# Two-layer hybrid encoder on one core: a weight sum, memory's operand and a low part drawn later, and one head's scaling on another engine

## The chip, the core and the metric

The kernel runs on one core of a Trainium2 chip. Its engines work side by side, each with its own queue in program order: TensorE (PE: matmuls and transposes; PEld is its weight load), VectorE (DVE), ScalarE (ACT), GpSimd (POOL) and SyncE (SP, which here only issues transfers). An instruction starts when everything ahead of it in its queue has been started and what it reads and writes is free. The metric is the device time of one execution in microseconds (us); lower is better.

## What is computed

The input is x, 512 tokens by 1024, and 256 memory tokens by 1024. There are two layers, all in 32-bit floats. Layer 0 attends in dilated windows (24 heads of 128 in three groups of eight), layer 1 with grouped queries (8 query heads on 2 key heads, rotated along two axes). Both also attend to memory with 4 heads. One projection of the normalised x feeds heads, memory queries and a SiLU gate; the gated heads go through an output projection and are added to x.

```
for i in range(DEPTH):
    h = rmsnorm(x, norm_g[i])
    mem_h = rmsnorm(mem, mem_norm_g[i])
    proj = jnp.einsum('bsd,de->bse', h, w_in)
...
    o_mem = memory_attention(q_mem, mem_h, w_mem_kv[i], mem_qn_g[i], mem_kn_g[i])
    y = jnp.concatenate([o_mix, o_mem], axis=-1) * jax.nn.silu(gate)
    x = x + jnp.einsum('bse,ed->bsd', y, w_out[i])
```

In layer 0 the three groups of a head are weighed against each other by a softmax over their log-sums: o = sum over g of w_g * o_g. The kernel keeps the scores of a head in two tiles `prob[o]` of 128 x 4 x 256: the first group (o = 0) and the two dilated ones side by side (o = 1).

## The kernel before

**Products in three passes.** A matmul of full 32-bit precision is made of three: each operand is split into a high part (rounded to the format fp32r) and a low part (what is left). `mm_early` and `mm_late` (L172, L173, L176) issue them: high by high, low by high, then high by low. For a weight, ScalarE draws the high part `wh` (L307, a cast of a 128x1024 piece) and VectorE the low part `wo` (L317, a subtraction). Activations are split the same way, by `split` (L160, L163) and by `put` (L567, L568).

**Seven products for eight.** Most projections (kinds W2, W1, W1b and their like) use a scheme of seven block products: the weights' quarters 21, 11, 12, 22 are combined into sums T1, T2, T3, T4. They are used in the order 21, 11, T1, T2, 22, T3, T4, each against one combination of activations (`PRODUCTS`: "12", "11", "S1", "S2", "S4", "S3", "22"). `s_chunk` runs them. Two accumulation banks take turns: the product with S2 is added to the bank of product 11, after `add` (L401) has read that bank, and the product with S4 to the bank of S1, after `keep` (L384) has.

**Weights.** The class `Weights` keeps the order of all this by hand. A step is one call of `advance`, made after each group of matmuls. In a step it draws low parts that are due (`lo`), issues at most one sum (`sum`), draws one or two high parts (`hi`), and issues loads (`dma`, on SP's queue, L258) as long as fewer pieces are live than `KEEP` says. T1 is summed on VectorE in layer 0 (L276) and by an adding transfer in layer 1 (L272); T2, T3 and T4 are adding transfers, issued by GpSimd (L281, L286, L291). T2 and T4 add one tile in on-chip memory to another (`wl<-wl`), T3 a piece of `wall`. A sum is issued no earlier than `LEAD` = 2 steps after the one that it needs; T4 needs T2 and the tile of quarter 21, whose low part must have been drawn one step before. A piece's tile is given back when its last user has been issued.

**Side work.** `Driver` runs everything else as generators, a piece of each per tick; a tick follows each step. `spawn(gen, n)` starts one n ticks later, and a `yield n` lets n ticks pass. `late` puts a piece at the end of the tick. The tiles of 128x1024 floats (tag m4: weights, activations, memory's tiles) share 23 places.

**Order around the change.** The list `PLAN` is worked through as `SEQ` orders it: memory's keys and values of layer 0 (8 steps), the plain values (14), memory's queries (7, chunk 3), the eight heads (14 each; head 0 is chunk 4), three gate chunks (7 each), the output projection (14, chunk 15, steps 162 to 175) with its last quarter (O1: 8 steps, 176 to 183), then layer 1: memory's keys and values (T2b: 8), memory's queries (W1bs: 7, chunk 20, steps 192 to 198), the rest (W1b, W2b, O1).

- Memory's queries (`ev_qm`): squares summed on ScalarE (L592), mse and rstd on GpSimd (L448, L449), the multiply on VectorE (L597), four transposes (L1073).
- `attn_a(h)` is the attention of head h of layer 0, spread over ticks. Its end: the factors `c`, `scale(1)`, two ticks later `scale(0)` and `turn(1)` (eight transposes, L1244), then `turn(0)`, `pv(1)` (L1265) and `pv(0)`. Head 7's end falls into the output projection, where VectorE also prepares the operands y (`prep_y`: L875, L890 to L905, casts L874).
- `mem_norm(1)`, spawned as the output projection begins, loads memory and its gains (L617, L634), four ticks later multiplies the first half (L495, two of them), one tick later the second half, and transposes and splits both (L501, L160, L163) in this and the next tick. Its result is read by the T2b steps.
- `rest_t` forms the activations S2, S4, S3, 22 of layer 1 (L571, L577; split by L567, L568) while the T2b and W1bs steps run.

Of the kernel before, what the change touches and what calls it, by code (L numbers as in the profile page):

```python
# [12 lines left out]
AF = mybir.ActivationFunctionType  # L13
ALU = mybir.AluOpType
# [7 lines left out]
TCKW = {}  # L22
NBIG, NM4, NS2, SCRATCH = 7, 23, 14, 2048
RING, LEAD = 4, 2
BULK, ACTIVE, SET_AT, WARM, MEM_B, PREP_Y, ACC_AT, PREP_B, HALF, SET_B = 2, 2, 15, 1, 12, 1, 4, 1, {"a": 3, "b": 3, "o": 0}, 9
MEM_STEP = 1, 1
MEM_D = 4
DIRECT, DIRECT_B = (7,), (6, 7)
# [8 lines left out]
PLAN = ["W2"] + ["T2"] * 2 + ["W1", "W2s"] + ["W2" if c.isdigit() else "W1" for c in A_ORDER[1:]] + ["W2"] + ["O1"] * 2 + ["T2b"] * 2 + ["W1bs"] + ["W1b"] * 6 + ["W2b"] + ["O1"] * 2  # L37

SEQ = [1, 2, 0] + list(range(3, len(PLAN)))
T1_DMA = 17  # L40
KEEP = {"T2": 8, "T2b": 6, "O1": 6, "W1": 9, "W2": 10, "W2s": 9, "W1bs": 9, "W1b": 7, "W2b": 9}

# [85 lines left out]
def trunk_kernel(ctx: ExitStack, tc: tile.TileContext, x, mem, wall, norm_g, mem_norm_g, gcol,  # L128
                 qn_a, kn_a, qn_b, kn_b, ident_d, mask_d, tab_a, tab_b, out):
    nc = tc.nc  # L130
    V, A, G, T = nc.vector, nc.scalar, nc.gpsimd, nc.tensor
# [11 lines left out]
    def m4(dt=F32, name="m4"):  # L143
        return pool.tile([128, 1024], dt, tag="m4", name=name, bufs=NM4)
# [43 lines left out]
    def pieces(kind):  # L188

        return 2 * GROUPS[kind][0] if kind in GROUPS else 4 if kind in ("W1", "W1b", "W1bs") else 8  # L190

    class Weights:
        def __init__(self):
            self.items, self.last, self.need, self.allocs, self.sums = [], [], [], [], []
            self.users = {}
            g = 0
            for c in SEQ:
                kind, d = PLAN[c], sum(pieces(k) for k in PLAN[:c])
                base = len(self.items)
                if kind in GROUPS:  # L200
                    units, nb = GROUPS[kind]
                    if kind == "O1":
                        n = PLAN[c - 1] == "O1"
                        for x in range(2):
                            self.items.append((c, "P", x))
                            self.last.append(g + 5)
                            self.allocs.append(((c, "P", x), d + x, kind))
                            self.users[c, "P", x] = 1
                        self.need += [base + 2] * 2 if not n else [base + 2] * 6
                        g += 2 if not n else 6  # L210
                        units = 0
                    for u in range(units):
                        for x in (2 * u, 2 * u + 1):
                            self.items.append((c, "P", x))
                            self.last.append(g + (u + 1) * nb - 1)
                            self.allocs.append(((c, "P", x), d, kind))
                            self.users[c, "P", x] = 1
                            d += 1
                        self.need += [base + 2 * u + 2] * nb
                    g += units * nb  # L220
                else:
                    n = 1 if kind in ("W1", "W1b", "W1bs") else 2
                    at = {k: d + i * n for i, k in enumerate(("21", "11", "12", "22"))}
                    self.allocs += [((c, k, x), at[q] + x, kind) for k, q in LOADS for x in range(n)]
                    for k in ORDER:
                        for x in range(n):
                            self.items.append((c, k, x))
                            self.last.append(g)
                            self.need.append(len(self.items))
                            if k[0] == "T":  # L230
                                self.sums.append(((c, k, x), at["11" if k == "T1" else "22"] + x))
                            if k != "T4":
                                self.users[c, k, x] = 1 if k in ("22", "T3") or k == "11" and c >= T1_DMA else 2
                            g += 1
            assert sum(pieces(k) for k in PLAN) == wall.shape[0]
            self.g = -1
            self.live = 0
            self.tile, self.load_at, self.at, self.lo_at = {}, {}, {}, {}
            self.n_hi = self.n_lo = self.taken = 0
            self.op, self.hi_at = [], []  # L240
# [22 lines left out]
        def sum(self, force=False, want=None):  # L263

            for n, (key, d) in enumerate(self.sums[:8]):
                if want and key != want:
                    continue
                c, k, x = key
                if k == "T1" and c >= T1_DMA:
                    if not self.ripe(self.load_at, key, force):  # L270
                        continue
                    G.dma_start(self.tile[key], wall[d], accum_op=ALU.add)  # L272
                elif k == "T1":
                    if not (self.ripe(self.load_at, key, force) and self.ripe(self.at, (c, "11", x), force)):
                        continue
                    V.tensor_tensor(self.tile[key], self.tile[key], self.tile[c, "11", x], ALU.add)  # L276
                    self.use((c, "11", x))
                elif k == "T2":
                    if not (self.ripe(self.load_at, key, force) and self.ripe(self.at, (c, "T1", x), force, 1 if c < T1_DMA else None)):
                        continue  # L280
                    G.dma_start(self.tile[key], self.tile[c, "T1", x], accum_op=ALU.add)  # L281
                    self.use((c, "T1", x))
                elif k == "T3":
                    if not self.ripe(self.load_at, key, force):
                        continue
                    G.dma_start(self.tile[key], wall[d], accum_op=ALU.add)  # L286
                else:
                    if not (self.ripe(self.lo_at, (c, "21", x), force, 1) and self.ripe(self.at, (c, "T2", x), force)):
                        continue
                    self.tile[key] = self.tile[c, "21", x]  # L290
                    G.dma_start(self.tile[key], self.tile[c, "T2", x], accum_op=ALU.add)  # L291
                    self.use((c, "T2", x))
                self.at[key] = self.g
                self.sums.pop(n)
                return True
            return False

        def hi(self, force=False):
            i = self.n_hi
            if i >= len(self.items) or not self.ripe(self.at, self.items[i], force, 1 if self.items[i][1] == "T1" and self.items[i][0] < T1_DMA else None):  # L300
                return False
# [31 lines left out]
        def advance(self):  # L333

            self.g += 1
            for _ in range(2):
                if self.n_lo < self.n_hi and self.hi_at[self.n_lo] < self.g:
                    self.lo()
            self.sum()
            if self.hi():  # L340
                self.hi()
            self.dma()
            if self.g + 1 < len(self.need):
                self.ready(self.need[self.g + 1])
# [787 lines left out]
    def attn_a(h, qk0, qs, ks, v12, n_done):  # L1132
# [3 lines left out]
        prob = [m4(name="p").rearrange("p (b k) -> p b k", b=4) for _ in range(2)]  # L1136
# [10 lines left out]
        for o in range(2):  # L1147
            new = []
            for b2 in range(2):
                sp = at("sa").rearrange("p (b k) -> p b k", b=2)  # L1150
                mine = []
                for i in range(2):
                    b = 2 * b2 + i
                    cs = slice(b * 128, (b + 1) * 128)
                    if o == 0:
                        lo, hi = max(0, 128 * b - 64), min(S, 128 * b + 192)
                        c0 = lo - (128 * b - 64)
                        c1 = c0 + hi - lo
                        T.matmul(sp[:, i, c0:c1], qk0[:, 0, cs], qk0[:, 1, lo:hi], start=True, stop=True, skip_group_check=True)  # L1159
                    else:  # L1160
                        c0, c1 = 0, 256
# [58 lines left out]
        V.reciprocal(rd, dn)  # L1220
        c = small.tile([128, 2, 4], F32, tag="c", name="c", bufs=2)
        V.tensor_tensor(c.rearrange("p o b -> p (o b)"), e[:, 0], rd, ALU.mult)
        yield 1

        pts = {}
# [2 lines left out]
        def scale(o):  # L1228
            for b in range(4):
                c0, c1 = (64 if o == 0 and b == 0 else 0), (192 if o == 0 and b == 3 else 256)  # L1230
                V.tensor_scalar(prob[o][:, b, c0:c1], prob[o][:, b, c0:c1], c[:, o, b:b + 1], 0.5, ALU.mult, ALU.mult)

        def turn(o):

# [24 lines left out]
        def pv(o):  # L1259
# [19 lines left out]
            drv.late(comb)  # L1279

        scale(1)
        yield Y[6]
        scale(0)
        turn(1)
        yield Y[7] + (h == 7)
# [10 lines left out]
    for c in A_ORDER:  # L1296
        if c.isdigit():
            drv.later(attn_a(int(c), *head_chunk(int(c))))
        else:
            if c == "b":  # L1300
                drv.spawn(prep_y(), PREP_Y)
            gate(H, *{"m": (8, 0), "a": (0, 1), "b": (4, 2)}[c])
# [334 lines left out]
```

## Time and profile before

| | us |
|---|---|
| median of 3 runs | 959.88 |
| lowest, highest | 959.16, 960.65 |
| profiled execution | 960.29 |
| span of its trace (first to last instruction) | 958.4 |

The granted TensorE clock was 1.000 over the whole span. The largest groups of the page are VectorE's low parts and ScalarE's high parts, then the matmuls:

```profile
L317 DVE TENSOR_TENSOR wo<-wl,wh 128x1024 fp32r<-128x1024 f32 x255 | 316.0, 1245 | 5.6 <-ACT wh L307 5.5
L307 ACT CAST wh<-wl 128x1024 fp32r<-128x1024 f32 x255 | 268.5, 1059 | 34.5 <-PE pj L173 16.9
L172 PE MATMUL pj<-wh,hS 128*128 128x512 f32 (+1 forms) x448 | 157.4, 365 | 1.6 <-ACT hS L567 1.6
```

How to read the rows. A group gives line, engine, operation, output<-inputs, shapes, count, then the busy time in us and the mean of one in ns, then the idle time of the engine just ahead of it and what ended most of that. A row of waits gives the waiting instruction, what released it, the total in us, how often, and the longest. A row of the timeline gives start and duration in us, then the instruction or a run of like ones (x3), and in brackets the idle time before it. Each duration overlaps the next one's start a little. A releaser is inferred from what ended last and can be another than the true one. An engine that waits costs nothing unless the one that sets the end waits for it.

### The profile page before, as it was taken

How to read it: one execution, taken by the hardware profiler on the slowest of the kernel's cores; microseconds unless marked ns; L12 is line 12 of the kernel's file. 1: busy time of each engine (PE TensorE's matmuls, PEld its weight loads, DVE VectorE, ACT ScalarE, POOL GpSimd, SP SyncE). 2: the span in 40 equal slices, each digit the busy share in tenths (PEclk: the TensorE clock that was granted, in tenths of full speed). 3: DMA queues.
4: the chain of work that ended last, by engine and by line, in shares of the span. 5: the costliest groups of instructions: out<-in, count | busy, mean ns of one | idle time of the engine just before them, and what ended most of it. 6: DMA issues, size and time to landing. Idle time of an engine off the chain costs nothing.

```text
span 958.4 us, 16597 instructions
## 1 busy us (share of the span) xinstructions
PE 944.6 (99%) x5682; PEld 831.9 (87%) x5682; DVE 791.7 (83%) x1415; ACT 678.0 (71%) x1693; POOL 332.7 (35%) x478
## 2 busy tenths in 40 slices
PE   8999999999999999999999999999999999999998
PEld 4879888888888888888889997878999999998886
DVE  4999586888888888979788999977988898769893
ACT  5875689686868686767775766537778876879770
POOL 1412423557454546463726111113232330011110
PEclk9999999999999999999999999999999999999999
DMA  9989946868787969696877989889885687787824
GB/s 354 320 193 344 304 111 173 291 133 258 152 260 156 262 154 264 154 259 138 234 185 185 268 204 308 280 250 328 230 189 117 190 237 173 210 207 187 248 54 127
DMA packets 87897, 208.23 MB, mean 217 GB/s; under 512 B 25219, under 2 KB 35203, under 8 KB 87813
## 3 DMA queue, kind: packets, MB, share of 16 engines
q1 hardware_dynamic: 68660, 144.18, 44.1%
q0 software_dynamic: 17856, 60.83, 34.2%
q10 hardware_dynamic: 1296, 2.16, 0.6%
q8 instruction: 45, 0.74, 0.3%
q14 instruction: 40, 0.32, 0.1%
HBM read 156.48 MB, written 11.86 MB: 176 GB/s over the span
## 4 chain that ended last, share of the span: by engine, by line
PE 90%; DVE 4%; DMA 3%; ACT 2%; issue 1%; POOL 0%; DVEq 0%; ACTq 0%; POOLq 0%
PE pj L173 24%; PE pj L172 23%; PE pj L176 23%; PE qT L604 2%; PE pt L1244 2%; PE sa L1163 1%; PE oo L1265 1%; PE sa L1159 1%; PE ptb L1467 1%; DMA og<-odb 1%; DVE wo L317 1%; PE xT L501 1%; PE ob L176 1%; PE row L625 1%; PE pmt L734 1%
## 5 line engine op out<-in xcount | busy, mean ns | idle before, releaser
L317 DVE TENSOR_TENSOR wo<-wl,wh 128x1024 fp32r<-128x1024 f32 x255 | 316.0, 1245 | 5.6 <-ACT wh L307 5.5
L307 ACT CAST wh<-wl 128x1024 fp32r<-128x1024 f32 x255 | 268.5, 1059 | 34.5 <-PE pj L173 16.9
L172 PE MATMUL pj<-wh,hS 128*128 128x512 f32 (+1 forms) x448 | 157.4, 365 | 1.6 <-ACT hS L567 1.6
L173 PE MATMUL pj<-wh,hS 128*128 128x512 f32 (+1 forms) x448 | 152.0, 353 | 0.0
L172 PE MATMUL pj<-wh,h 128*128 128x512 f32 (+1 forms) x336 | 117.9, 364 | 0.0
L173 PE MATMUL pj<-wh,h 128*128 128x512 f32 (+1 forms) x336 | 114.0, 353 | 0.0
L449 POOL TENSOR_TENSOR rstd<-mse,half 128x4 f32<-128x4 f32 (+2 forms) x96 | 100.5, 1046 | 8.0
L176 PE MATMUL pj<-wo,hS 128*128 128x512 f32 (+1 forms) x448 | 100.0, 352 | 0.2 <-DVE wo L317 0.2
L172 PEld LDWEIGHTS pj<-wh,hS 128*128 128x128 f32 x448 | 84.8, 189 | 12.1 <-ACT wh L307 1.8
L173 PEld LDWEIGHTS pj<-wh,hS 128*128 128x128 f32 x448 | 84.9, 190 | 10.2
L384 ACT COPY sn<-pj 128x512 f32<-128x512 f32 x132 | 73.2, 590 | 25.9 <-PE pj L176 23.7
L176 PEld LDWEIGHTS pj<-wo,hS 128*128 128x128 f32 x448 | 74.6, 189 | 12.4 <-DVE wo L317 0.6
L448 POOL TENSOR_SCALAR mse<-hss 128x4 f32<-128x4 f32 (+1 forms) x86 | 42.4, 493 | 123.0 <-ACT junk L592 118.6
L592 ACT ACTIVATE junk<-sn 128x128 f32<-128x128 f32 x264 | 79.1, 308 | 4.8 <-DVE sn L395 4.7
L1107 POOL TENSOR_TENSOR ta<-sn,tabs 128x128 f32<-128x128 f32 (+1 forms) x64 | 36.6, 579 | 119.5 <-DVE sn L597 92.4
L401 DVE TENSOR_TENSOR sn<-pj,sn 128x512 f32<-128x512 f32 x99 | 67.3, 683 | 9.2 <-PE pj L176 6.5
L176 PE MATMUL pj<-wo,h 128*128 128x512 f32 (+1 forms) x336 | 74.8, 352 | 0.0
L173 PEld LDWEIGHTS pj<-wh,h 128*128 128x128 f32 x336 | 63.7, 190 | 7.5
L172 PEld LDWEIGHTS pj<-wh,h 128*128 128x128 f32 x336 | 63.7, 189 | 7.5 <-DVE sn L401 0.2
L291 POOL DMA_DIRECT2D wl<-wl x33 | 29.1, 881 | 116.0 <-DVE wo L317 67.8
L176 PEld LDWEIGHTS pj<-wo,h 128*128 128x128 f32 x336 | 56.0, 189 | 8.8
L597 DVE TENSOR_TENSOR sn<-sn,rstd 128x512 f32<-128x512 f32 (+1 forms) x82 | 47.8, 592 | 7.9 <-POOL rstd L449 7.9
(240 smaller groups left out, 2328.6 us busy)
## 6 DMA issues: line engine op xcount, KB each, us to landing
wl<-in_wall_dram SPq DMA_DIRECT2D x222, 512.0 KB, 7.4
wl<-wl POOLq DMA_DIRECT2D x66, 512.0 KB, 5.6
wl<-in_wall_dram POOLq DMA_DIRECT2D x42, 512.0 KB, 8.4
acc<-sn POOLq DMA_DIRECT2D x16, 256.0 KB, 5.7
od<-o SPq DMA_DIRECT2D x11, 256.0 KB, 5.7
og<-od SPq DMA_DIRECT2D x10, 256.0 KB, 7.6
odb<-o SPq DMA_DIRECT2D x10, 256.0 KB, 3.2
og<-odb SPq DMA_DIRECT2D x10, 256.0 KB, 4.7
```

The lines of the kernel that those rows point to most:

```text
L172: T.matmul(o, a, b, start=start, stop=False, skip_group_check=True)
L173: T.matmul(o, c, d, start=False, stop=False, skip_group_check=True)
L176: T.matmul(o, a, b, start=False, stop=stop, skip_group_check=True)
L307: A.copy(wh, self.tile[self.items[i]])
L317: V.tensor_tensor(wo, self.tile[key], wh.bitcast(F32), ALU.subtract)
L384: A.copy(t, b)
L401: V.tensor_tensor(t, b, t, ALU.subtract if q == "12" else ALU.add)
L448: G.tensor_scalar(e, ss, EPS, None, ALU.add)
L449: G.tensor_tensor(r, e, half[:, 0:n], ALU.pow)
L592: A.activation(jk, p[:, j * 128:(j + 1) * 128], AF.Square, scale=QS, accum_out=ss[:, j:j + 1])
L597: V.tensor_tensor(xn[:, 0:n], p.rearrange("p (a b) -> p a b", a=4)[:, 0:n], r[:, 0:n, None].to_broadcast([128, n, 128]), ALU.mult)
L1107: G.tensor_tensor(ta[:, 0:n], xn[:, 0:n, 0:32], ropeA[:, 0, b, s0:s0 + n], ALU.mult)
```

## The change

Four edits.

1. `T4_AT = {4: 4}`: for chunk 4 (head 0) T4 is summed no earlier than 4 steps after T2 instead of 2.
2. `MEM_B` 12 to 14: `mem_norm(1)` starts two ticks later.
3. In a step of a chunk of kind W1bs, `advance` draws at most one low part that is due, instead of two. `kinds` holds the kind of each step for this.
4. For h == 7 the scaling of the scores' exponentials is done by ScalarE, a copy with a factor per row, instead of VectorE. The constant 0.5 goes into `c` by one more VectorE instruction on 128x8.

```diff
-BULK, ACTIVE, SET_AT, WARM, MEM_B, PREP_Y, ACC_AT, PREP_B, HALF, SET_B = 2, 2, 15, 1, 12, 1, 4, 1, {"a": 3, "b": 3, "o": 0}, 9
+BULK, ACTIVE, SET_AT, WARM, MEM_B, PREP_Y, ACC_AT, PREP_B, HALF, SET_B = 2, 2, 15, 1, 14, 1, 4, 1, {"a": 3, "b": 3, "o": 0}, 9
...
+T4_AT = {4: 4}
...
-            self.users = {}
+            self.users, self.kinds = {}, []
...
+                self.kinds += [kind] * (g - len(self.kinds))
...
-                    if not (self.ripe(self.lo_at, (c, "21", x), force, 1) and self.ripe(self.at, (c, "T2", x), force)):
+                    if not (self.ripe(self.lo_at, (c, "21", x), force, 1) and self.ripe(self.at, (c, "T2", x), force, T4_AT.get(c))):
...
-            for _ in range(2):
+            for _ in range(1 if self.kinds[self.g] == "W1bs" else 2):
                 if self.n_lo < self.n_hi and self.hi_at[self.n_lo] < self.g:
                     self.lo()
...
+        if h == 7:
+            V.tensor_scalar(c, c, 0.5, None, ALU.mult)
         yield 1
...
-                V.tensor_scalar(prob[o][:, b, c0:c1], prob[o][:, b, c0:c1], c[:, o, b:b + 1], 0.5, ALU.mult, ALU.mult)
+                pb = prob[o][:, b, c0:c1]
+                if h == 7:
+                    A.activation(pb, pb, AF.Copy, scale=c[:, o, b:b + 1])
+                else:
+                    V.tensor_scalar(pb, pb, c[:, o, b:b + 1], 0.5, ALU.mult, ALU.mult)
```

## The prediction

> **What bounds the kernel now.** I read the page first, then the waits of TensorE, then the timeline of the other engines around each of those waits.
>
> ```profile
> span 958.4 us, 16597 instructions
> PE 944.6 (99%) x5682; PEld 831.9 (87%) x5682; DVE 791.7 (83%) x1415; ACT 678.0 (71%) x1693; POOL 332.7 (35%) x478
> PE pj L172 <- ACT hS L567: 1.6, 1, 1.6
> PE qT L1073 <- DVE sn L597: 0.9, 1, 0.9
> PE pt L1244 <- DVE p L1231: 0.9, 2, 0.5
> PE pj L173 <- DVE wo L317: 0.8, 1, 0.8
> ```
>
> TensorE sets the end: 944.6 of 958.4 us, so at most 13.8 us can be had without taking matmuls away. The change removes none. It can gain only where TensorE waits, and these four rows are four such places. Each edit touches the engine queue ahead of one of them. So I cost each edit at its stall. A tick is one round of the side work after a group of matmuls (a step).
>
> **Edit 1, T4_AT (head 0's fourth sum, L291).** Counting the steps by PLAN (8 of memory, 14 of v0, 7 of qm), head 0 begins at step 29. Following the rules of the class, its T2 sums are issued in steps 26 and 27 and its T4 sums in 28 and 29, two steps later each. GpSimd runs in order, and the T4 add reads what the T2 add writes.
>
> ```profile
> 96.90 1.82 POOL L281 DMA_DIRECT2D wl<-wl  x2
> 104.33 0.19 ACT L592 ACTIVATION_READ_ACCUMULATOR junk<-sn 128x1 f32 x1
> 107.42 0.85 POOL L291 DMA_DIRECT2D wl<-wl  x1 [8.70 <-PE pj L176]
> 108.66 1.05 POOL L449 TENSOR_TENSOR rstd<-mse,half 128x4 f32<-128x4 f32 x1
> 109.74 0.69 DVE L597 TENSOR_TENSOR sn<-sn,rstd 128x512 f32<-128x512 f32 x1 [5.13 <-POOL rstd L449]
> 110.48 0.66 PE L1073 MATMUL qT<-ident,sn 128*128 128x128 f32 x4 [0.94 <-DVE sn L597]
> ```
>
> The first T4 add holds GpSimd idle for 8.70 us. The page names a matmul as releaser, but that had long ended; I read it as the T2 add landing, 10 us after its issue. Behind it stands the normalisation of qm: its squares were summed at 104.52, its rstd came at 109.71, and so VectorE idled 5.13 us and TensorE 0.94 us. With 4 instead of 2, the T4 adds go to steps 30 and 31, behind that rstd in the queue. From the end of the issue (108.27) to the end of rstd is 1.44 us, so rstd would end at 104.52 + 1.44 = 106.0, the multiply at 106.7, and the transposes are ready 3.8 us before TensorE comes to them (109.5). The T3 adds still follow in steps 32 and 33, no load moves (T2's tile is freed by its low part in step 33, later than either), and T4's sum is first read in step 38, some 20 us on. The T4 issue costs its 0.85 us wherever it stands, now before nothing that TensorE waits for. Gain 0.94; bounds 0 (T2 lands so late that the add still blocks a norm) and 1.2.
>
> A rule speaks against moving this issue: the Trainium skill, "SBUF — State Buffer", section "A bandwidth-pool intuition that's wrong (but worth ruling out)", says that a transfer issued by GpSimd is starved while certain VectorE instructions hold the shared port, about 3.1 us in place of 0.62. VectorE is idle at the old place and busy at the new one. By that rule the edit would give back about 2.5 us of GpSimd time, which the 3.8 us of slack above would still cover. The second T4 add, issued with VectorE busy, is no evidence of it here.
>
> **Edit 2, head 7's scaling to ScalarE (L1231).** Eight instructions leave VectorE, eight of the same shape go to ScalarE, and one 128x8 product is added. VectorE has no gap in this stretch and runs two steps behind, so both transposes of head 7 (L1244) reach TensorE before the scaled tile.
>
> ```profile
> 588.56 1.07 PE L176 MATMUL pj<-wo,yS 128*128 128x512 f32 x4
> 592.92 1.07 PE L176 MATMUL pj<-wo,yS 128*128 128x512 f32 x4
> 595.64 1.07 PE L176 MATMUL pj<-wo,yS 128*128 128x512 f32 x4
> 600.50 1.07 PE L176 MATMUL pj<-wo,yS 128*128 128x512 f32 x4
> 589.12 1.13 DVE L1231 TENSOR_SCALAR p<-p,c 128x256 f32<-128x256 f32 x4
> 596.65 1.06 DVE L1231 TENSOR_SCALAR p<-p,c 128x192 f32<-128x192 f32 x4
> 584.22 2.95 ACT L307 CAST wh<-wl 128x1024 fp32r<-128x1024 f32 x3
> 588.04 1.22 ACT L874 CAST yS<-yf 128x512 fp32r<-128x512 f32 x2 [0.87 <-DVE yf L900]
> 595.56 1.22 ACT L874 CAST yS<-yf 128x512 fp32r<-128x512 f32 x2 [2.32 <-DVE yf L905]
> 128.12 0.91 ACT L725 ACTIVATE pm<-pm,rdm 128x256 f32<-128x256 f32 x2
> 620.09 1.08 PE L176 MATMUL pj<-wh,y 128*128 128x512 f32 x4
> 621.00 1.04 PE L501 MATMUL xT<-ident,m 128*128 128x128 f32 x8
> 623.71 1.07 PE L176 MATMUL pj<-wh,y 128*128 128x512 f32 x4
> ```
>
> A step with eight transposes that wait for nothing takes 623.71 - 620.09 = 3.62 us. Head 7's two take 592.92 - 588.56 = 4.36 and 600.50 - 595.64 = 4.86: lost are 0.74 and 1.24, together 1.98, more than the 0.9 that the wait rows name, because the waits between single transposes count as busy. On ScalarE the first scaling stands between the second and third of the three casts, from about 586.4. At 0.91/2 = 0.46 each, four take 1.8 us and end at 588.2, before the transposes at 589.5. The third cast and the two L874 move back by up to 1.3; the second scaling, two steps on, takes another 1.8 from about 591.6 and ends near 593.4, well before 596. Added are 3.6 us; the two idle stretches of ScalarE, 0.87 and 2.32, take 3.2 of them, and its next wait is for PE anyway. What ScalarE brings late (casts read two steps on, two copies out of PSUM read at 597) has 2 us or more. If that cover were gone, each late copy would hold TensorE by what is left of 3.6. VectorE, 2.2 us lighter, draws its low parts earlier. Gain 1.98; bounds: -1 (ScalarE late by what its gaps do not hold, with nothing won) and 2.2.
>
> The Trainium skill, "ScalarE: Activation LUTs", section "Rules for kernel authors", sends multiplies to VectorE, not ScalarE. The rows agree on the price (0.46 against 0.28 us each). By that rule alone the sum would be a loss of 8 x 0.18 = 1.4 us; on rows alone rival B below covers it.
>
> **Edit 3, MEM_B 12 to 14.** `mem_norm(1)` moves by two ticks: three loads on SP, four multiplies (L495), sixteen transposes, four copies and four low parts (L163).
>
> ```profile
> L495 DVE SCALAR_TENSOR_TENSOR m<-m,rm,row x4: 745/746/747, 619.5 to 623.8; 128x512 f32<-128x512 f32 x4
> 624.50 1.28 DVE L163 TENSOR_TENSOR act<-xT,act 128x512 fp32r<-128x512 f32 x2
> 626.30 1.22 DVE L317 TENSOR_TENSOR wo<-wl,wh 128x1024 fp32r<-128x1024 f32 x1
> 627.57 0.50 PE L173 MATMUL pj<-wo,y 128*128 128x512 f32 x1 [0.77 <-DVE wo L317]
> 632.21 0.69 DVE L766 TENSOR_TENSOR acc<-pj,acc 128x512 f32<-128x512 f32 x1 [2.03 <-PE pj L176]
> 605.35 2.53 SPq L258 DMA_DIRECT2D wl<-in_wall_dram  x3
> 605.35 17.04 SPq L258 DMA_DIRECT2D wl<-in_wall_dram  x4
> m<-in_mem_dram SPq DMA_DIRECT2D x2, 512.0 KB, 6.9
> SPq L258 <- DVE m L495: 10.5, 1, 10.5
> ```
>
> The last low part of the out projection (626.30 to 627.52) stops TensorE for 0.77. Ahead of it on VectorE stand the four L495 (2.8) and two L163 (1.28). Two ticks later all of them come behind it: it ends about 4 us earlier, at 623.6, and TensorE, whose 16 transposes move too, needs it at 624.9. The moved work falls among steps where VectorE idles 2.03 of each 2.72 us, with no low part drawn, and is needed only eight steps on. On SP the three loads now follow two weight loads. Those and the next one were issued without delay by 607.9; only the fourth waited (to 622.1, for memory's own tile). So the loads still go by 607.9 and land near 615. Gain 0.77; bounds: 0.8 and, if the loads had to wait, rival C.
>
> **Edit 4, one low part per step in W1bs.** Only its first step draws two (T1's and T2's); T2's goes one step on, and so does one weight load (a step early enough: its sum is formed three steps later).
>
> ```profile
> 674.51 2.35 DVE L317 TENSOR_TENSOR wo<-wl,wh 128x1024 fp32r<-128x1024 f32 x2
> 677.38 1.46 DVE L568 TENSOR_TENSOR hS<-f,hS 128x512 fp32r<-128x512 f32 x2
> 678.76 0.68 DVE L401 TENSOR_TENSOR sn<-pj,sn 128x512 f32<-128x512 f32 x1
> 679.59 0.36 PE L172 MATMUL pj<-wh,hS 128*128 128x256 f32 x1 [1.64 <-ACT hS L567]
> ```
>
> The S2 product adds to the bank that L401 has to read first. L401 ends at 679.44 and TensorE starts at 679.59, so I take L401, not the named cast, as what was late. In the new order T2's low part still stands ahead of L401, one place later. It only fills a hole: the two L568 take 1.46 where two such take 1.28 (the L163 row). Gain 0.18; bounds 0 and 1.1 (one low part, if the cast is the true releaser). Late next is the same L401.
>
> **Sum.** 0.94 + 1.98 + 0.77 + 0.18 = 3.87 us, about 3.9. On the profiled span 958.4 gives 954.5. The profiled execution took 960.29, 1.89 more than its span and 0.41 above the median of 959.88; I take the difference off the median: **956.0 us**.
>
> **Rivals.** A: the boundary of the layers does not move with TensorE, and takes back what was won ahead of it.
>
> ```profile
> 646.25 1.07 ACT L160 CAST h<-xT 128x512 fp32r<-128x512 f32 x2 [1.57 <-PE xT L501]
> 660.42 0.69 DVE L597 TENSOR_TENSOR xn<-pj,rstd 128x512 f32<-128x512 f32 x1 [1.25 <-POOL rstd L449]
> ```
>
> For it: from 660.42 VectorE is nearly without a gap up to L401, and sets that place. Against: that run begins with GpSimd's rstd, and behind it ScalarE's casts at 646.25, which waited for TensorE; so it shifts with TensorE. If it stood still, edits 2 and 3 (2.75) would be lost there: 959.88 - 1.12 = 958.8. B: ScalarE late gives back edit 2 whole: 959.88 - 1.89 = 958.0. For it the 3.6 us added, against it the gaps. C, the slower side: the loads of memory, now behind two weight loads, get their tiles only when the fourth load got its own (622.1). They land at 622.1 + 6.9 = 629.0, or 630.5 for the last; the first L495 pair (1.4) ends near 631, while TensorE stands at the transposes after its step, at 626.4. It loses 4.6, and edit 3's 0.77 is lost on top if the multiplies stand ahead of a low part: 956.0 + 5.4 = 961.4. It decides from a landing later than 625. Against it: three loads had free tiles by 607.9. D: the change does not do what it says, each stall comes back behind the next producer: 959.9.
>
> **Chances.** Forecast 0.62, A 0.10, B 0.13, C 0.08, D 0.07. Two runs of this kernel can be told apart from about 0.2%, 1.9 us, so faster means below 958.0. The forecast and most of B are faster: 0.73. A, D and a part of B are within: 0.18; C and mishaps unseen: 0.09. The range runs from 955.0 (edit 4 at its upper bound, 0.9 more) to 958.8 (A).
>
> **What would show it.** In the changed profile GpSimd's mse follows ScalarE's sum near 104.5 without an 8.7 us wait, and the row of L1073 among TensorE's waits is gone; the steps with L1244 take 3.62; L173 does not wait for L317 near 626, and SP issues memory's loads before 608; the wait at the S2 product stays at about 1.5. The prediction is wrong if that last wait grows to 4, if `keep` copies on ScalarE (L384) stop matmuls near 597, or if L501 waits for L495.

## The result, and the profile after

| | before | changed |
|---|---|---|
| median of ten runs, us | 960.43 | 957.11 |
| lowest, highest | 959.16, 962.67 | 955.56, 959.05 |
| profiled execution | 960.29 | 959.05 |
| span of its trace | 958.4 | 957.3 |

The ratio is 0.9962, 95% interval 0.995 to 0.9974: the change saves 3.65 us, between 2.5 and 4.8. The forecast was 956.0 with a range from 955.0 to 958.8. A second set of five runs gave 956.05 against 959.91, measured beside it (ratio 0.996, 0.9947 to 0.9972). The execution that was profiled first is the slowest of its ten, 1.94 us above their median, and its trace holds a loss that a second profile of the same kernel does not have; it is found below.

The page of the changed kernel, its span and its engines' busy times:

```profile
span 957.3 us, 16591 instructions
PE 943.8 (99%) x5682; PEld 832.1 (87%) x5682; DVE 790.0 (83%) x1408; ACT 681.4 (71%) x1701; POOL 336.2 (35%) x478
```

ScalarE is 3.4 us longer (predicted 3.6), VectorE 1.7 shorter (predicted 2.2); in the second profile it is 2.4 and 2.6, so these totals vary by about 1 us. TensorE has the same 5682 instructions. Two of TensorE's waits in the changed kernel:

```profile
PE pj L173 <- ACT sn L386: 2.4, 2, 1.5
PE pt L1252 <- DVE p L1239: 0.3, 1, 0.3
```

The rows for the transposes of `sn` (0.9) and for the low part of the out projection (0.8) are gone. The row of `pt` is another one: 0.3 at head 6, near 547, where VectorE still scales; head 7 has none left. The 2.4 of `keep` (L386) are the S2 product (1.5) and a stop of 0.94 that was not there before. The lines have moved by one to eight: L1252 is the transpose L1244, L403 the `add` L401, L386 the `keep` L384, L319 the low part L317, L503 and L497 are L501 and L495.

What a stop costs is read best from one step's last group of matmuls to the next one's. In the timelines from here on, most rows between those shown are left out. First the timeline of TensorE of before, rows that the prediction did not show:

```profile
108.48 1.07 PE L176 MATMUL pj<-wo,h 128*128 128x512 f32 x4
112.92 1.07 PE L176 MATMUL pj<-wo,h 128*128 128x512 f32 x4
...
626.41 0.39 PE L172 MATMUL pj<-wh,y 128*128 128x512 f32 x1
627.91 0.39 PE L172 MATMUL pj<-wh,y 128*128 128x512 f32 x1
628.37 1.08 PE L176 MATMUL pj<-wh,y 128*128 128x512 f32 x4
...
676.83 1.12 PE L176 MATMUL pj<-wo,hS 128*128 128x256 f32 x8
681.57 1.12 PE L176 MATMUL pj<-wo,hS 128*128 128x256 f32 x8
```

The timeline of TensorE in the changed kernel, at the same places, in order the fourth sum, head 7, memory's operand, the S2 product:

```profile
108.33 1.07 PE L177 MATMUL pj<-wo,h 128*128 128x512 f32 x4
109.24 0.60 PE L1075 MATMUL qT<-ident,sn 128*128 128x128 f32 x4
111.53 1.08 PE L177 MATMUL pj<-wo,h 128*128 128x512 f32 x4
...
584.29 0.50 PE L173 MATMUL pj<-wh,yS 128*128 128x512 f32 x1 [0.94 <-ACT sn L386]
589.00 1.07 PE L177 MATMUL pj<-wo,yS 128*128 128x512 f32 x4
589.91 1.03 PE L1252 MATMUL pt<-ident,p 128*128 128x128 f32 x8
592.61 1.07 PE L177 MATMUL pj<-wo,yS 128*128 128x512 f32 x4
595.33 1.07 PE L177 MATMUL pj<-wo,yS 128*128 128x512 f32 x4
596.24 1.03 PE L1252 MATMUL pt<-ident,p 128*128 128x128 f32 x8
598.94 1.07 PE L177 MATMUL pj<-wo,yS 128*128 128x512 f32 x4
...
623.96 1.07 PE L177 MATMUL pj<-wh,y 128*128 128x512 f32 x4
624.88 1.03 PE L503 MATMUL xT<-ident,m 128*128 128x128 f32 x8
627.58 1.07 PE L177 MATMUL pj<-wh,y 128*128 128x512 f32 x4
...
674.20 1.12 PE L177 MATMUL pj<-wo,hS 128*128 128x256 f32 x8
676.81 0.36 PE L173 MATMUL pj<-wh,hS 128*128 128x256 f32 x1 [1.50 <-ACT sn L386]
678.79 1.12 PE L177 MATMUL pj<-wo,hS 128*128 128x256 f32 x8
```

The step with the transposes of `sn` takes 3.20 where it took 4.44. Both steps with head 7's transposes take 3.61 (4.36 and 4.86 before). The steps with memory's transposes take 3.62, where the second of them took 4.66, and the step of the S2 product 4.59 for 4.74.

To see the gain grow, each TensorE instruction of a trace was paired with the same one of before, and the difference of their starts taken at the ends of each stretch. The table gives how much later (+) or earlier (-) TensorE comes out of a stretch than it went in, against the trace of before, in us. The stretches are named by the time in before; the kernels other than the changed one are those of the experiments.

| kernel | 105-114 (edit 1) | 540-588 | 588-605 (edit 2) | 618-634 (edit 3) | 670-683 (edit 4) | 860-920 |
|---|---|---|---|---|---|---|
| changed, first profile | -1.23 | +1.74 | -2.00 | -1.07 | -0.14 | +1.65 |
| changed, second profile | -1.22 | +0.02 | -2.00 | -1.07 | -0.17 | +0.68 |
| edit 1 alone | -1.23 | +0.10 | -0.02 | +0.05 | +0.01 | -0.63 |
| edit 2 alone | -0.08 | +0.02 | -2.00 | 0.00 | +0.01 | +1.98 |
| edit 3 alone | -0.18 | +0.83 | 0.00 | -1.07 | +0.02 | -1.12 |
| edit 4 alone | +0.24 | +0.02 | 0.00 | +0.02 | -0.16 | +1.02 |
| low part behind the add | -1.22 | +0.42 | -2.00 | -1.08 | -0.71 | +0.53 |

In each of four stretches exactly the kernels with that edit gain, and the same amount each time; the first column varies by up to 0.24 in the kernels without its edit, the other three by up to 0.05. The two other stretches differ from one trace to the next, and between the two profiles of one kernel.

### The profile page after: what moved, and what is told of

The parts are those of the page before. It is cut to its first block, busy times and chain, and to the rows that moved or that the text cites. A ratio compares the mean times of both kernels' runs of the same rounds, so it can differ in the third digit from the quotient of the medians.

```text
span 957.3 us, 16591 instructions
## 1 busy us (share of the span) xinstructions
PE 943.8 (99%) x5682; PEld 832.1 (87%) x5682; DVE 790.0 (83%) x1408; ACT 681.4 (71%) x1701; POOL 336.2 (35%) x478
## 4 chain that ended last, share of the span: by engine, by line
PE 83%; DMA 6%; DVE 5%; ACT 4%; issue 1%; POOL 0%; SPq 0%; DVEq 0%; POOLq 0%; ACTq 0%
PE pj L174 22%; PE pj L173 22%; PE pj L177 21%; PE qT L606 2%; DVE wo L319 2%; DMA og<-od 1%; PE sa L1165 1%; PE oo L1273 1%; PE pt L1252 1%; DMA wl<-in_wall_dram 1%; PE ptb L1475 1%; PE sa L1161 1%; DMA acc<-sn 1%; PE xT L503 1%; PE row L627 1%
## 5 line engine op out<-in xcount | busy, mean ns | idle before, releaser
L319 DVE TENSOR_TENSOR wo<-wl,wh 128x1024 fp32r<-128x1024 f32 x255 | 316.3, 1246 | 6.8 <-ACT wh L309 6.6
L386 ACT COPY sn<-pj 128x512 f32<-128x512 f32 x132 | 73.2, 590 | 26.0 <-PE pj L177 22.9
L450 POOL TENSOR_SCALAR mse<-hss 128x4 f32<-128x4 f32 (+1 forms) x86 | 45.1, 525 | 126.0 <-ACT junk L594 121.7
L403 DVE TENSOR_TENSOR sn<-pj,sn 128x512 f32<-128x512 f32 x99 | 67.4, 684 | 9.1 <-PE pj L177 6.4
L594 ACT ACTIVATION_READ_ACCUMULATOR junk<-sn 128x1 f32 x264 | 51.8, 196 | 0.0
```

Of the source, the lines that this page charges most:

```text
L319: V.tensor_tensor(wo, self.tile[key], wh.bitcast(F32), ALU.subtract)
L386: A.copy(t, b)
L403: V.tensor_tensor(t, b, t, ALU.subtract if q == "12" else ALU.add)
L450: G.tensor_scalar(e, ss, EPS, None, ALU.add)
L594: A.activation(jk, p[:, j * 128:(j + 1) * 128], AF.Square, scale=QS, accum_out=ss[:, j:j + 1])
```

## The experiments

### Each edit alone

Fourth sum:

```diff
+T4_AT = {4: 4}
...
-self.ripe(self.at, (c, "T2", x), force)
+self.ripe(self.at, (c, "T2", x), force, T4_AT.get(c))
```

> Edit 1 alone. My theory: GpSimd no longer waits 8.7 us ahead of head 0's first T4 add, TensorE comes 1.1 us earlier past the transposes at 110 us and keeps it to the end: about 959.3, 1.1 below the kernel before. Rival (the gain is lost where the gates read head outputs): by coming earlier TensorE makes VectorE wait longer for a read of head outputs near 537 us (3.13 us in the changed kernel, 0.88 before), VectorE is late up to 590 us, and TensorE loses about 1.6 us near 548 and 584 us: no gain, 960.4 or above. If the longer wait is chance, it need not be there in this run.

Median 959.84 against 959.97; ratio of the paired runs 0.9984 (0.9969 to 0.9999), about 1.5 us. TensorE gains 1.23 at the place and keeps it to 860. It does not stop near 584, so an earlier TensorE alone does not bring that stop.

The scaling on ScalarE:

```diff
+        if h == 7:
+            V.tensor_scalar(c, c, 0.5, None, ALU.mult)
...
+                if h == 7:
+                    A.activation(pb, pb, AF.Copy, scale=c[:, o, b:b + 1])
+                else:
+                    V.tensor_scalar(pb, pb, c[:, o, b:b + 1], 0.5, ALU.mult, ALU.mult)
```

> Edit 2 alone. My theory: the two steps with head 7's transposes take 3.62 us each in place of 4.36 and 4.86, TensorE is 1.9 us earlier at 600 us, and the time is about 958.5. Rival (ScalarE gives it back): copies out of PSUM on ScalarE hold TensorE between 584 and 600 us by as much, and the time stays at 960.4.

Median 959.35, ratio 0.9991 (0.9978 to 1.0005). The trace gains 2.00 at the place, nothing near 584, and loses 1.98 in the tail: in this one execution the whole gain is gone again. The time alone could not have shown that the edit works.

Memory's operand:

```diff
-..., MEM_B, ... = ..., 12, ...
+..., MEM_B, ... = ..., 14, ...
```

> Edit 3 alone. My theory: the wait of TensorE near 627 us goes, TensorE is 0.8 to 1.2 us earlier from 632 us on, and the wait at the S2 product near 679 us keeps its 1.6: time about 959.4. Rival (the boundary does not move): the wait at the S2 product grows to about 2.7 and the time stays at 960.4.

Median 958.97, ratio 0.9995 (0.9981 to 1.001). The place gives 1.07. This kernel stops near 584 as well, with VectorE still scaling head 7, and the step with that stop lies ahead of everything that its edit moves. TensorE's timeline of edit 3 alone:

```profile
584.34 0.50 PE L172 MATMUL pj<-wh,yS 128*128 128x512 f32 x1 [0.63 <-ACT sn L384]
```

One low part in a step:

```diff
-            for _ in range(2):
+            for _ in range(1 if self.kinds[self.g] == "W1bs" else 2):
```

> Edit 4 alone. My theory: VectorE's add of product 11 is what TensorE waits for at the S2 product, and the moved low part still stands ahead of it; the wait goes from 1.64 to about 1.45 us, time 960.2, no measurable change. Rival (the named cast on ScalarE is the releaser): the wait shrinks by up to 1.1 us, time about 959.3.

Median 959.84, ratio 0.9999 (0.9988 to 1.0009). TensorE's timeline of edit 4 alone, at the S2 product:

```profile
679.11 0.36 PE L172 MATMUL pj<-wh,hS 128*128 128x256 f32 x1 [1.48 <-ACT sn L385]
```

The wait is 1.48 for 1.64, and the stretch gains 0.16: the small gain of the forecast, not the 1.1 of its upper bound.

Of the four ratios only the first one's interval stays below 1. Where an edit is worth 0.2 to 2 us and single executions spread over 3 to 6 us, the times bear the sum and the traces the parts.

### The changed kernel again

No edit: the same kernel in five rounds.

> The changed kernel once more, unaltered. My theory: the loss of 1.16 us at 584 us and the losses of about 2 us between 903 and 915 us in the first profile come from single transfers of head outputs that took longer (VectorE's wait for the read near 537 us, 3.13 us, and near 900 us, 4.43 us), which differ from execution to execution; here the waits differ again, while the gains at 110, 600 and 632 us (1.1, 1.9, 1.2) come out the same. Rival: the losses belong to the changed order and are there again, about 3 us in all. Time 956.5 to 957.5 either way.

Median 956.05 (955.65 to 957.2), profiled execution 956.56. The four places give 1.22, 2.00, 1.07 and 0.17 once more; the loss from 540 to 588 is absent. The row of VectorE that goes with it stands before the gated heads, where VectorE waits for a head's output read back from device memory. VectorE's timeline of the first profile of the changed kernel, then of before, then of the second profile:

```profile
537.80 0.69 DVE L830 TENSOR_TENSOR yf<-sn,og 128x512 f32<-128x512 f32 x1 [3.13 <-DMA og<-od]
...
900.70 0.69 DVE L830 TENSOR_TENSOR sn<-sn,og 128x512 f32<-128x512 f32 x1 [4.43 <-DMA og<-odb]
```

```profile
536.84 0.69 DVE L828 TENSOR_TENSOR yf<-sn,og 128x512 f32<-128x512 f32 x1 [0.88 <-DMA og<-od]
...
902.66 0.69 DVE L828 TENSOR_TENSOR sn<-sn,og 128x512 f32<-128x512 f32 x1 [3.08 <-DMA og<-odb]
```

```profile
535.51 0.69 DVE L830 TENSOR_TENSOR yf<-sn,og 128x512 f32<-128x512 f32 x1 [0.73 <-DMA og<-od]
...
898.94 0.69 DVE L830 TENSOR_TENSOR sn<-sn,og 128x512 f32<-128x512 f32 x1 [4.31 <-DMA og<-odb]
```

Near 537 the wait ranks the traces: with 0.7 to 1.0 (before, edits 1, 2 and 4 alone, the second profile, and the last two kernels below) TensorE does not stop near 584; with 1.83 (low part behind the add) it stops for 0.20, with 2.25 (edit 3 alone) for 0.63, with 3.13 for 0.94. VectorE comes late out of the wait, and what stands behind it reaches ScalarE, and so the `keep` copy, late: against the second profile, VectorE of the first is 2.30 us later at 537.80 and still 1.58 later at 582.23, and the two `keep` copies begin at 583.67 where they began at 582.09. Two profiles of the same kernel have 3.13 and 0.73, so here it is the transfer and not the program that differs.

Near 900 it is less clean. The two traces with short waits (2.49 with edit 3, 2.68 with edit 1) gain 1.12 and 0.63 in the tail, those of 3.9 and more lose 0.7 to 2.0; in between, a wait of 3.48 (low part behind the add) goes with a loss of 0.53 and one of 3.17 (T4 three steps behind, below) with 1.33. The wait accounts for one slice of the tail: from 903 to 909 TensorE's loss against before is the wait less the 3.08 of before, within 0.1 us, in all nine traces. The rest of the tail, from 860 to 880 (-0.53 to +0.29) and from 909 to 920 (-0.04 to +0.93), was not traced to a cause. The wait itself may not be chance: the three traces with neither edit 2 nor edit 4 have the three shortest (2.49, 2.68, 3.08), and the same kernel has 4.43 and 4.31 in its two profiles. Whether an edit lengthens it stays open.

### The low part behind the add

On top of the changed kernel: step 192 draws one low part, step 193 none, so that T2's comes behind `add`; every other step may again draw two.

```diff
-            for _ in range(1 if self.kinds[self.g] == "W1bs" else 2):
+            for _ in range({192: 1, 193: 0}.get(self.g, 2)):
```

> The changed kernel with T2's low part drawn yet one step later, behind the add of product 11 on VectorE (the second step of W1bs draws none). My theory: that add is what TensorE waits for at the S2 product; it comes 1.13 us earlier, the wait of 1.50 us falls to about 0.4, and the time is about 1.1 us below the changed kernel's. Rival (a copy or cast on ScalarE is what is late): the wait stays at 1.5 and so does the time.

Median 955.75 (955.02 to 955.99), ratio 0.9953 (0.9941 to 0.9965). It is the fastest median of the study, though its interval overlaps that of the changed kernel; the gain at the place, 0.71 for 0.17, is seen in the trace, about half of what was expected. First VectorE's timeline of the changed kernel, then the timelines of VectorE, ScalarE and TensorE of this one:

```profile
674.24 1.22 DVE L319 TENSOR_TENSOR wo<-wl,wh 128x1024 fp32r<-128x1024 f32 x1
675.98 0.69 DVE L403 TENSOR_TENSOR sn<-pj,sn 128x512 f32<-128x512 f32 x1
```

```profile
673.22 0.69 DVE L570 TENSOR_TENSOR hS<-f,hS 128x512 fp32r<-128x512 f32 x1 [0.50 <-ACT hS L569]
673.83 0.68 DVE L403 TENSOR_TENSOR sn<-pj,sn 128x512 f32<-128x512 f32 x1
```

```profile
671.60 1.06 ACT L309 CAST wh<-wl 128x1024 fp32r<-128x1024 f32 x1
672.55 0.63 ACT L569 CAST hS<-f 128x512 fp32r<-128x512 f32 x1
```

```profile
674.66 0.35 PE L173 MATMUL pj<-wh,hS 128*128 128x256 f32 x1 [0.92 <-ACT hS L569]
```

In both kernels TensorE starts 0.14 to 0.15 us after the add ends (676.67 and 676.81; 674.51 and 674.66), as in before (679.44 and 679.59), while the profile names `keep` in one and a cast in the other. With edit 4 alone it is 0.14 too (678.97 and 679.11). So the add is the releaser. Leaving out a low part of 1.22 brings TensorE only 0.54 forward, because VectorE then waits 0.50 for the cast of S4 on ScalarE, which stands behind a weight's cast. That cast is what is late next.

### Three steps, and T1 by a transfer

On top of the changed kernel, one execution:

```diff
-T4_AT = {4: 4}
+T4_AT = {4: 3}
```

> The changed kernel with head 0's T4 sums 3 steps behind T2 in place of 4. My theory: what counts is that the first T4 add stands behind the norm of memory's queries in GpSimd's queue, and one step does that: TensorE does not wait at 110 us, just as with 4. Rival (the landing of the T2 add has to be past): GpSimd blocks on the add up to 107 us again, the next norm is late and part of the 1.1 us is lost.

956.83. TensorE gains the same 1.22 at the place. GpSimd's timeline of this kernel:

```profile
106.60 0.93 POOL L293 DMA_DIRECT2D wl<-wl  x1 [0.94 <-PE pj L177]
110.36 0.86 POOL L293 DMA_DIRECT2D wl<-wl  x1 [2.83 <-DVE wo L319]
111.29 0.23 POOL L450 TENSOR_SCALAR mse<-hss 128x4 f32<-128x4 f32 x1
```

Both adds stand behind the first norm, and the second one again holds GpSimd for 2.83 us with a norm behind it; the row names a low part, but the second T2 add landed at 109.77, just ahead of the issue. That stop takes nothing from TensorE here. What counts is that the first norm is not behind an add, not by how much.

Finally, on top of the kernel with the low part behind the add, T1's sums are made by adding transfers, not by VectorE, already from chunk 15 on, the output projection, and not from chunk 17; the aim was slack for the stop near 584. The same constant also makes T2's sum and T1's high part in that chunk wait two steps instead of one.

```diff
-T1_DMA = 17
+T1_DMA = 15
```

> As the kernel with the later low part, and T1 of the output projection of layer 0 is summed by an adding transfer in place of VectorE (two instructions of 1.22 us less on VectorE near 556 and 561 us, two more transfers of 512 KB). My theory: VectorE is behind from 537 to 590 us whenever the read of head outputs is late; 2.4 us less there keep TensorE from waiting at 548 to 584 us: up to 1 us below the kernel with the later low part in executions with a late read, 0.5 in the median. Rival: the transfers land late, TensorE waits for T1's high part near 578 us and the time is 1 us or more above.

956.07 (955.24 to 956.85), ratio 0.9956 (0.9944 to 0.9969): no different from the kernel without it. In the profiled execution the wait near 537 was short (0.71), so it says nothing on the stop that it was to cover.

## Why the prediction was right, step by step

**Edit 1** went as forecast, and its size was off: 1.23 for 0.94, just above the upper bound of 1.2. GpSimd's timeline of the changed kernel:

```profile
104.47 0.23 POOL L450 TENSOR_SCALAR mse<-hss 128x4 f32<-128x4 f32 x1 [5.89 <-ACT junk L594]
104.79 1.05 POOL L451 TENSOR_TENSOR rstd<-mse,half 128x4 f32<-128x4 f32 x1
107.07 0.93 POOL L293 DMA_DIRECT2D wl<-wl  x1 [1.23 <-PE pj L177]
...
109.27 1.87 POOL L451 TENSOR_TENSOR rstd<-mse,half 128x4 f32<-128x4 f32 x1
111.11 0.91 POOL L293 DMA_DIRECT2D wl<-wl  x1
```

The norm's rstd ends at 105.84 (forecast 106.0), with no T4 add ahead of it. The long wait was read rightly as the landing of the T2 add: in the trace of before the two T2 adds landed at 106.40 and 110.18, and the T4 adds went at 107.42 and 110.76. In the changed kernel the first T2 add landed at 106.39 and the T4 add went at 107.07, now behind the norm. The slack was written as 3.8 us; from the prediction's own numbers, 109.5 and 106.7, it is 2.8. The issues took 0.93 and 0.91 with VectorE busy on both, against 0.85 at the old place. The starving that the Trainium skill describes in "SBUF — State Buffer", section "A bandwidth-pool intuition that's wrong (but worth ruling out)", does not appear in these two issues.

**Edit 2** is the term that fits best, 2.00 for 1.98, and the only one taken from the distances of steps, not from a wait row. ScalarE's timeline of the changed kernel:

```profile
586.90 1.72 ACT L1237 ACTIVATE p<-p,c 128x256 f32<-128x256 f32 x4 [0.28 <-DVE c L1226]
...
591.97 1.60 ACT L1237 ACTIVATE p<-p,c 128x192 f32<-128x192 f32 x4
```

The scalings cost 1.72 and 1.60 (forecast 1.8 each) and end at 588.62 and 593.57, 1.3 and 2.7 us ahead of the transposes (589.91 and 596.24). Nothing that ScalarE brought late stopped TensorE between 586 and 605, so rival B falls. The sign of failure that the prediction named, a stop by `keep` near 597, showed itself at 584: before the first scaling, and in a kernel without edit 2 too. The Trainium skill, "ScalarE: Activation LUTs", section "Rules for kernel authors", sends multiplies to VectorE, and the traces agree on the price: ScalarE took 3.32 us for what VectorE did in 2.19. But price did not decide here: VectorE was late and ScalarE had the time.

**Edit 3** works as forecast, and again 0.30 more: 1.07 for 0.77, above its upper bound of 0.8. SyncE's timeline of before, then of the changed kernel, then VectorE's of the changed kernel:

```profile
603.77 1.36 SPq L634 DMA_DIRECT2D m<-in_mem_dram  x2
```

```profile
603.92 1.13 SPq L636 DMA_DIRECT2D m<-in_mem_dram  x2
```

```profile
620.90 1.22 DVE L319 TENSOR_TENSOR wo<-wl,wh 128x1024 fp32r<-128x1024 f32 x1
622.03 1.41 DVE L497 SCALAR_TENSOR_TENSOR m<-m,rm,row 128x512 f32<-128x512 f32 x2
```

Memory's loads are issued at 603.92 to 605.05, as early as before (603.77 to 605.13), and the multiplies start without a wait: rival C falls. The last low part ends at 622.12, ahead of the first multiply and 2.8 us before TensorE's transposes at 624.88.

**Edit 4** gives 0.14 to 0.17 for 0.18. The reading of the releaser, the add and not the cast that the row names, is confirmed from both sides: by the small gain of the edit, and by the larger one once the low part stands behind the add. In the changed kernel the same add is late next, as forecast; with the low part out of its way it is ScalarE's cast.

**What was mis-sized.** Both short terms were read from a row of waits. Such a row counts the idle time from the modelled end of the matmul before. In the rows of before, the matmul at 626.41 is given 0.39 us, yet the next like it normally starts after 0.23 (a group of four takes 1.08, not four times 0.39); so the stop that ended at 627.57 cost 1.16 - 0.23 = 0.93, not 0.77, and the one after it came after 0.34 (627.91), another 0.11 late. Together that is 1.04. At the fourth sum it is the same: 110.48 - 108.48 is 2.00, with the transposes ready it is 109.24 - 108.33 = 0.91, so 1.09 are lost ahead of them for a named 0.94, and 0.15 behind them.

**The sum.** Forecast 3.87; in place 1.22 + 2.00 + 1.07 + 0.17 = 4.46 (second profile). The times give 3.65 (2.5 to 4.8) and, by the second set's medians, 3.86. So the terms gave 0.6 more than forecast, and up to 0.8 came back elsewhere. That the forecast sum lies so near the measured saving is partly luck: terms sized too small against a loss elsewhere that the forecast did not have. The forecast's time is 1.1 us under the median, and half of that is the base: it counted from 959.88, the median of three runs, where ten gave 960.43.

Part of what came back is the stop near 584, which three of the ten traces have. Whether the tail also takes back a part by rule stays open. All five traces that have all four edits lose 0.5 to 1.7 there (the three in the table, 1.33 with T4 three steps behind, 1.71 with T1 by a transfer), but so do edits 2 and 4 alone, and the trace of before, against which that is counted, is itself one execution. The intervals hold the full 4.46 as well.

**Rivals.** A, the boundary taking back what was won: from 605 to 683 TensorE keeps every gain, and the S2 wait is 1.50, not 4. B and C fell above. D falls with the four stretches.

## What to carry to other kernels

Price a stop of the bounding engine by the distance of its steps, stalled against unstalled, and not by the row of waits: here the rows were 0.3 us short at each of the two stops that were priced by them. When a releaser in a row had long ended, look for the instruction whose end stands the same small distance ahead of the start in several traces (here 0.14 to 0.15 us), and move that one. For edits of a tenth of a per cent, align the trace of each kernel with that of before and read the place; profile the same kernel twice before explaining a loss elsewhere.

## What the runs showed of the hardware

- Reading back a head's output held VectorE for 0.73 or 3.13 us at the same place of the same kernel, and for 2.49 to 4.45 us near 900 over the kernels of the table. With the first pair went 1.7 us of TensorE's time from 540 to 588 (+0.02 and +1.74 in the table).
- GpSimd's rstd on 128x4 took from 1.04 to 2.07 us within the trace of the changed kernel. It took 1.05 at 104.79, and 1.87 at 109.27, with two low parts on VectorE from 107.88 to 110.23 in the row below. A low part beside it does not decide this alone: at 719.28 it took 1.04 with one beside it for nine tenths of the time, at 473.38 it took 1.87 with none. Why was not tried. VectorE's timeline of the changed kernel:

```profile
107.88 2.35 DVE L319 TENSOR_TENSOR wo<-wl,wh 128x1024 fp32r<-128x1024 f32 x2
```
